# Changing the load order, the first norm's path and the last columns of a planned two-block kernel

## The chip, the cores and the metric

The kernel runs on one core of one Trainium2 chip. The metric is the device time of one execution in microseconds (us); 773.08 us is the median of the runs of the kernel before.

## The reference, cut to what matters

A sequence of 256 rows of width 1024 (x) goes through two transformer blocks in float32. The first block has two layers; each normalises x, projects it, runs several kinds of attention (global with rotary positions, windowed, neighbourhood, and attention to a memory of 256 rows), gates the result and adds an output projection. The second block has a mixer, a cross attention and a squared-ReLU MLP, and ends with a norm. Two places matter here. The first is the start of the first layer:

```
h = rmsnorm(x, norm_gain[0])                 # y = x * rsqrt(mean(x*x) + 1e-6) * g
qa, ka, va, qb, kb, vb, qm, gate = split_cols(h @ w_in_even, SPLIT_EVEN)
```

The second is the end of the MLP and the final norm:

```
x = x + squared_relu_mlp(rms_norm(x, g_mlp), w_up, w_down)
return rms_norm(x, g_final)
```

## The kernel before, in words

**Numbers.** Every float32 operand of a product is split in two: a high half, rounded to the fast float32 format (`t_wh` for weights, `t_gh`, `t_hT`, `t_mT`, `t_yh` for activations), written by ScalarE (ACT), and a low half, the remainder (`t_wl` and so on), written by VectorE (DVE). A product of two split operands is three matmuls, high by high, high by low and low by high (`mm3`), or two instructions where high and low activations stand side by side. So each load of weights (`t_raw`, three buffers of up to 1 MB, loaded over SP's queue) needs one instruction of ScalarE and one of VectorE before TensorE (PE; its weight loads are PEld) can finish with it, and a `raw` buffer comes free when VectorE has written the low half.

**Who sets the order.** The kernel's methods do not issue anything; `Plan.record` notes each instruction with what it depends on. `Plan.order` then plays the program through with a table of costs: at each step it takes the engine that can start earliest, and on it the ready instruction with the lowest priority number, which is the place in the program plus `bias`. A transfer is given 450 ns on its queue, and its bytes at 358 bytes per ns on one common bus. The engines and queues get their instructions in that fixed order, so a wrong guess of a time shows on the chip as an engine that waits although other work of its own is ready. `either` lets the plan choose between VectorE and ScalarE for one step. `nc.ahead` lets a load be issued ahead of its place.

**The start.** `consts` loads the gains and the first two 128-row blocks of x transposed (`xT`, host-made input `x_t`), one over SP's and one over ACT's queue, and gives PE 24 matmuls on zeros (`t_warm`). `layer_even` does not wait for the norm's factor r (one per row of x): it multiplies the columns of x.T by the gain alone (`gain_t`, whose `turn(k)` makes the two halves `t_gh` for one block of 128), and sums q, k, v and the second k's neighbours for k = 0 to 7, 896 columns in four PSUM banks (`sweep`; 12 matmuls for each k). The factor r is applied to these results afterwards. `columns` issues the loads of two k at a time in the pieces of its list: rows j0 to j1 and columns d0 to d1. Behind each pair of k stands a load of further blocks of x.T (`load_x`); with k = 6 come the rows of x themselves. `rope_tables` loads tables after k = 2 and 3.

From the rows of x, two sums of squares for each half (`square_sum`, either engine), the sum plus epsilon and a power of -1/2 on GpSimd (POOL) give r (`rstd`). All of this is recorded with `bias` -200, 200 places ahead. The products that follow (the second attention's k, called kb here, then the gate, then more) need the normed x transposed and split (`hT`). The kernel before gets it without a transpose of x: `spread` writes r on the diagonal of two 128x128 tiles (`t_p<-t_cst,t_rstd`), multiplies them by ones on PE (`t_at<-t_p,t_ones`) and copies the result, r along the free axis in every partition (`t_y`); VectorE then makes eight products x.T times gain times r (`t_xs`), and four pairs of instructions split them (`t_hT`).

`turns` is another way, used by later norms: the normed rows (`t_xn`, made by `scaled`, either engine) are transposed on PE in 128x128 pieces (`t_at<-t_cst,t_xn`), and ScalarE and VectorE evacuate each pair of pieces into the two halves with the gain (`t_mT`).

**The end.** `down_last` does the last product for each half of the rows (tt = 0, 1). For tt = 1 the second 512 columns are cut in two, and the last 256 go through a PSUM tile of their own (`own`). After each piece come the residual on VectorE (`t_x<-t_mm,t_rstd,t_x`), a sum of squares (`square_sum`) and the product with the final gain (`t_xg<-t_x,t_gb`). Then r from the sums (VectorE), the power (POOL), the scaling by r on VectorE and ScalarE, and the stores. The order of a piece's steps on VectorE there is again the plan's.

Of the kernel before, what the change touches and what calls it, by code (L numbers as in the profile page):

```python
# [10 lines left out]
F32 = mybir.dt.float32  # L11
# [5 lines left out]
P = 128  # L17
# [12 lines left out]
class Plan:  # L30
# [13 lines left out]
    def __init__(self, nc):  # L44
        import concourse.bacc as bacc
        self.nc = nc
        self.names = bacc.Bacc("TRN2", target_bir_lowering=False, num_devices=1)
        self.ops, self.tiles, self.last, self.bias, self.ahead, self.table = [], {}, None, 0, False, 0.0
        for e in self.ENGINES:
            setattr(self, e, Plan.Engine(self, e))  # L50

# [31 lines left out]
    def record(self, engine, method, args, kwargs):  # L83
        op = dict(i=len(self.ops), engine=engine, method=method, args=args, kwargs=kwargs, deps={}, uses=set(),
                  bias=self.bias)
        outs = [v for v in args[:1] if isinstance(v, bass.AP)] + [kwargs[k] for k in ("out", "accum_out") if k in kwargs]
        ins = [v for v in args[1:] if isinstance(v, bass.AP)]
        ins += [v for k, v in kwargs.items() if k not in ("out", "accum_out") and isinstance(v, bass.AP)]
        op["kind"] = self.tiles[outs[0].tensor.name]["kind"] if self.mine(outs[0]) else None
        for write, vs in ((False, ins), (True, outs)):  # L90
            for v in vs:
                if not self.mine(v):
                    continue
                t, b = self.box(v)
                op["uses"].add(t["name"])
                bank = t["pool"].space == bass.MemoryType.PSUM
                for j, w, c in t["log"]:
                    if j == op["i"] or not (w or write):
                        continue
                    o = self.ops[j]  # L100
                    if bank and engine == o["engine"] == "tensor":
                        op["deps"].setdefault(j, 0.0)
                    elif b[0] < c[1] and c[0] < b[1] and b[2] & c[2]:
                        lat = self.latency(o["engine"], engine) if engine != o["engine"] or w and not write else 0.0
                        op["deps"][j] = max(op["deps"].get(j, 0.0), lat)
                t["log"].append((op["i"], write, b))
        if engine == "tensor":
            self.last = op["i"]
        elif method == "dma_start" and op["kind"] != "raw" and self.last is not None and not self.ahead:
            op["deps"].setdefault(self.last, 0.0)  # L110
        op["cost"], op["after"], op["bytes"] = self.cost(engine, method, args, kwargs, outs, ins)
        op["forms"] = [(engine, method, args, kwargs, op["cost"])]
        self.ops.append(op)
# [48 lines left out]
    def order(self, prio):  # L162
# [37 lines left out]
        while len(seq) < n:  # L200
# [19 lines left out]
            if o["bytes"]:  # L220
                if e != "gpsimd":
                    ring[e] = max(ring[e], t) + 450.0
                    avail[e] = (ring[e], i)
                    bus = max(bus, ring[e] + 650.0)
                else:
                    bus = max(bus, end[i] + 650.0)
                bus += o["bytes"] / 358.0
                done = bus + o["after"]
            self.done[i] = done
            seq.append(i)  # L230
# [77 lines left out]
class Kernel:  # L308
# [59 lines left out]
    def consts(self):  # L368
# [9 lines left out]
        warm = self.base.tile([P, S], F32R, name="warm")  # L378
        nc.vector.memset(warm.bitcast(F32), 0.0)
        self.xT = [self.slot([P, 4, S], "xT", F32) for _ in range(2)]  # L380
        for k, queue in enumerate((nc.sync, nc.scalar)):
            self.load_x(k, 1, queue)
        busy = self.psum("at")
        for _ in range(WARM):
            nc.tensor.matmul(busy[:, 0, :], warm[:, :P], warm, start=True, stop=True)
# [133 lines left out]
    def gain_t(self, src, key, fast=False):  # L519

        nc = self.nc
        f = Halves(lambda: self.slot([P, 2, 2, S], "gh"))

        def turn(k):
            v, g, h, l = src[k // 4][:, k % 4, :], self.gcol(key, k), f(0, k), f(1, k)
            if k == 0 and fast:
                nc.vector.tensor_scalar(h, v, g, None, ALU.mult)
            else:
                nc.scalar.activation(h, v, AF.Copy, scale=g)
            nc.vector.scalar_tensor_tensor(l, v, g, h.bitcast(F32), ALU.mult, ALU.subtract)  # L530

        return f, turn
# [475 lines left out]
    def layer_even(self):  # L1008
# [5 lines left out]
        def columns(k0, parts, raw=None):  # L1014


            if raw is None:
                raw = self.wp.tile([P, 2, 896], F32, tag="raw", name=self.name("raw"), bufs=3)
            for j0, j1, d0, d1 in parts:
                c = d0 if d0 < 768 else d0 + 640  # L1020
                nc.sync.dma_start(raw[:, j0:j1, d0:d1], w_in[(k0 + j0) * P:(k0 + j1) * P, c:c + d1 - d0]
                                  .rearrange("(k p) c -> p k c", p=P))
# [12 lines left out]
                             k == 0, k == KT - 1)  # L1035

        for k0 in range(0, KT, 2):
            raw = columns(k0, ((0, 1, 0, 512), (0, 2, 512, 768), (0, 2, 768, 896), (1, 2, 0, 512)) if k0 == 0 else
                          ((0, 2, 0, 768), (0, 2, 768, 896)) if k0 < 6 else ((0, 1, 0, 768), (0, 1, 768, 896)))
            if k0 < 6:  # L1040
                self.load_x(k0 + 2, 2, nc.sync)
            else:
                for t in range(2):
                    nc.ahead = True
                    nc.sync.dma_start(self.x[:, t, :], a["x"][0, t * P:(t + 1) * P])
# [10 lines left out]
        for c in range(2):  # L1056
            squares(c)
        r = self.rstd(ms)
        rb = self.spread(r, self.work("y", [P, S], YB))
        hT = Halves(lambda: self.slot([P, 2, 2, S], "hT"))  # L1060
        for c in range(2):
            t = self.slot([P, 4, S], "xs", F32)
            for k in range(4):
                nc.vector.scalar_tensor_tensor(t[:, k, :], self.xT[c][:, k, :], self.gcol("norm0", 4 * c + k), rb,
                                               ALU.mult, ALU.mult)
            for k in (0, 2):
                self.hilo(*hT.pair(4 * c + k), t[:, k:k + 2])
        nc.bias = 0
        self.sink = self.base.tile([P, 8], F32, name="sink")
        nc.sync.dma_start(self.sink, a["sink_b"].to_broadcast([P, 8]))  # L1070
# [258 lines left out]
    def mlp(self, ms):  # L1329
# [47 lines left out]
        def down_last(s, t):  # L1377
            parts = [list(self.wide(a["w_down_2"], 512 * s, 4, 512 * c)) for c in range(2)]
            parts = [[(k0, *self.split(v)) for k0, v in half] for half in parts]
            for tt in range(2):  # L1380
# [4 lines left out]
                for i, (c, b0, b1) in enumerate(cuts):  # L1385
# [16 lines left out]
                    xv = self.x[:, tt, cs]  # L1402
                    if own:
                        nc.vector.scalar_tensor_tensor(xv, o, r2[:, tt:tt + 1], xv, ALU.mult, ALU.add)
                    self.square_sum(xv, ms[:, i:i + 1])
                    held.append((xg[c][:, tt, bs], xv, gb[:, cs]))
                    if b1 - b0 == 512:
                        nc.vector.tensor_tensor(*held.pop(), ALU.mult)
                r = self.work("rstd", [P, 2], 4)[:, :1]
                nc.vector.scalar_tensor_tensor(r, ms[:, 0:1], EPS, ms[:, 1:2], ALU.add, ALU.add)  # L1410
                if tt == 1:
                    nc.vector.tensor_tensor(r, r, ms[:, 2:3], ALU.add)
                nc.gpsimd.tensor_tensor(r, r, self.mhalf[:, :1], ALU.pow)
                for v in held:
                    nc.vector.tensor_tensor(*v, ALU.mult)
                rows = slice(tt * P, (tt + 1) * P)
                v = [xg[c][:, tt, :] for c in range(2)]
                nc.vector.tensor_scalar(v[0], v[0], r, None, ALU.mult)
# [140 lines left out]
```

## Time and profile before

| | |
|---|---|
| median of 3 runs | 773.08 us (772.73 to 773.56) |
| profiled execution | 773.77 us |
| its span in the profile | 771.9 us |
| mean granted TensorE clock | 0.997 |
| PE, DVE, ACT, POOL busy | 99%, 80%, 69%, 9% of the span |
| moved by the DMA queues | 140.39 MB, 182 GB/s in the mean |

A row of the timeline gives the start in us from the span's start, the duration (of several merged instructions: from the first start to the last end), the engine, the operation, what it writes and reads, shapes, the count, and in brackets the idle time before it and what ended that. All instructions have line 284, the line of `issue`, so the tile names tell the groups apart. Matmuls overlap, and their ends are modelled.

### The profile page before, as it was taken

Reading aid. Unit: us, or ns where it says so; the run is one execution under the profiler, and the core shown is the slowest. Engines: PE = TensorE matmul, PEld = TensorE weight load, DVE = VectorE, ACT = ScalarE, POOL = GpSimd, SP = SyncE. Lnnn points to the kernel's source line nnn. Section 1 sums busy time; section 2 is a strip of 40 time slices with the busy share of each in tenths; the row PEclk is TensorE's granted clock in tenths of the full one; section 3 lists DMA queues with packets and bytes.
Section 4 is the critical chain, followed back from the end, with each engine's and each line's share of the span. In section 5 each row is a group of like instructions: output and inputs, shape, how many; then the busy total and the mean of one; then the engine's idle time right before and its main releaser. Section 6 shows DMA issues by size and latency. Waiting matters only on the chain.

```text
span 771.9 us, 11841 instructions
## 1 busy us (share of the span) xinstructions
PE 760.7 (99%) x4370; PEld 662.6 (86%) x4370; DVE 614.3 (80%) x1136; ACT 529.0 (69%) x1034; POOL 66.6 (9%) x98
## 2 busy tenths in 40 slices
PE   9999999999999999999999999999999999999996
PEld 7898888888888888888888898899988888888885
DVE  5999998988779789979998899886677665555655
ACT  5687986976678678757796788466556765555562
POOL 2140010000001511132001000100000000000000
PEclk9999999999999999999999999999999999999998
DMA  8893555445568854765456644356535665656541
GB/s 315 284 268 111 165 183 177 159 165 164 164 211 250 218 188 144 199 197 193 134 191 194 191 163 156 117 165 219 191 110 164 195 188 167 204 177 209 170 163 55
DMA packets 109145, 140.39 MB, mean 182 GB/s; under 512 B 3744, under 2 KB 80736, under 8 KB 109088
## 3 DMA queue, kind: packets, MB, share of 16 engines
q1 hardware_dynamic: 103184, 131.12, 52.7%
q0 software_dynamic: 5472, 8.10, 4.8%
q8 instruction: 34, 0.56, 0.3%
q10 hardware_dynamic: 432, 0.43, 0.2%
q14 instruction: 23, 0.19, 0.1%
HBM read 134.92 MB, written 1.05 MB: 176 GB/s over the span
## 4 chain that ended last, share of the span: by engine, by line
PE 82%; ACT 6%; DVE 6%; DMA 3%; issue 2%; SPq 0%; POOLq 0%; POOL 0%; ACTq 0%; DVEq 0%
PE t_mm L284 61%; PE t_at L284 21%; DVE t_wl L284 2%; DMA t_raw<-in_w_in_even_dram 2%; ACT t_p L284 2%; ACT t_wh L284 2%; ACT t_y L284 1%; DVE t_y L284 1%; DVE t_p L284 1%; DMA t_xT<-in_x_t_dram 0%; ACT t_ph L284 0%; SPq L284 0%; ACT t_sum L284 0%; DVE t_pl L284 0%; DVE t_tanh L284 0%
## 5 line engine op out<-in xcount | busy, mean ns | idle before, releaser
L284 DVE TENSOR_TENSOR t_wl<-t_raw,t_wh 128x1024 fp32r<-128x1024 f32 (+2 forms) x238 | 288.7, 1217 | 69.9 <-ACT t_wh L284 67.2
L284 ACT ACTIVATE t_wh<-t_raw 128x1024 fp32r<-128x1024 f32 (+2 forms) x238 | 249.7, 1054 | 78.7 <-PE t_mm L284 57.4
L284 PE MATMUL t_mm<-t_mT,t_wh 128*128 128x512 f32 x496 | 179.6, 401 | 0.0
L284 PE MATMUL t_mm<-t_mT,t_wl 128*128 128x256 f32 x496 | 131.0, 283 | 0.0
L284 PE MATMUL t_mm<-t_wh,t_yh 128*128 128x512 f32 (+1 forms) x288 | 113.3, 393 | 0.0
L284 PE MATMUL t_mm<-t_wl,t_yh 128*128 128x512 f32 (+1 forms) x288 | 112.3, 390 | 0.0
L284 PE MATMUL t_mm<-t_wh,t_yl 128*128 128x512 f32 (+1 forms) x288 | 111.9, 391 | 0.0
L284 PEld LDWEIGHTS t_mm<-t_mT,t_wh 128*128 128x128 f32 x496 | 91.0, 188 | 13.4
L284 PEld LDWEIGHTS t_mm<-t_mT,t_wl 128*128 128x128 f32 x496 | 93.2, 189 | 6.6
L284 PE MATMUL t_at<-t_mT,t_wh 128*128 128x512 f32 x240 | 86.0, 395 | 0.0
L284 ACT COPY t_sum<-t_mm 128x256 f32<-128x256 f32 x90 | 33.2, 369 | 51.8 <-PE t_mm L284 51.3
L284 PE MATMUL t_mm<-t_wh,t_gh 128*128 128x256 f32 (+2 forms) x256 | 63.8, 333 | 0.0
L284 PEld LDWEIGHTS t_mm<-t_wl,t_yh 128*128 128x128 f32 x288 | 54.2, 188 | 10.7
L284 PEld LDWEIGHTS t_mm<-t_wh,t_yl 128*128 128x128 f32 x288 | 54.1, 188 | 10.6
L284 PEld LDWEIGHTS t_mm<-t_wh,t_yh 128*128 128x128 f32 x288 | 54.1, 188 | 10.3 <-ACT t_yh L284 0.3
L284 PE MATMUL t_at<-t_mT,t_wl 128*128 128x256 f32 x240 | 62.6, 280 | 0.0
L284 ACT ACTIVATE t_p<-t_p,t_st 128x256 f32<-128x256 f32 (+1 forms) x111 | 53.2, 494 | 10.6 <-DVE t_st L284 10.5
L284 PEld LDWEIGHTS t_at<-t_mT,t_wh 128*128 128x128 f32 x240 | 44.5, 188 | 8.3 <-issue 0.2
L284 DVE TENSOR_TENSOR t_sum<-t_mm,t_sum 128x256 f32<-128x256 f32 x90 | 37.9, 422 | 13.9 <-ACT t_sum L284 12.9
L284 PE MATMUL t_mm<-t_hT,t_wh 128*128 128x512 f32 (+1 forms) x160 | 48.3, 356 | 0.0
L284 PEld LDWEIGHTS t_at<-t_mT,t_wl 128*128 128x128 f32 x240 | 45.2, 188 | 3.5
L284 PE MATMUL t_mm<-t_gh,t_wh 128*128 128x512 f32 x128 | 47.3, 404 | 0.0
(189 smaller groups left out, 1371.7 us busy)
## 6 DMA issues: line engine op xcount, KB each, us to landing
t_raw<-in_w_in_odd_dram SPq DMA_DIRECT2D x20, 1024.0 KB, 5.2
t_raw<-in_w_up_dram SPq DMA_DIRECT2D x16, 1024.0 KB, 5.7
t_raw<-in_w_down_dram SPq DMA_DIRECT2D x16, 1024.0 KB, 5.0
t_raw<-in_w_in_dram SPq DMA_DIRECT2D x12, 1024.0 KB, 5.3
t_raw<-in_w_in_even_dram SPq DMA_DIRECT2D x10, 1024.0 KB, 5.1
t_raw<-in_w_mem_kv_dram SPq DMA_DIRECT2D x8, 1024.0 KB, 5.2
t_raw<-in_w_out_even_dram SPq DMA_DIRECT2D x6, 1024.0 KB, 5.2
t_raw<-in_w_out_odd_dram SPq DMA_DIRECT2D x6, 1024.0 KB, 5.9
```

Source lines behind the costliest of these rows:

```text
L284: f(*[self.real(v) for v in args], **{k: self.real(v) for k, v in kwargs.items()})
```

## The change

Five edits in one:

1. The second block of x.T is loaded over SP's queue, behind three pieces of the first weights, instead of over ACT's; `turn(1)`'s high half is made by VectorE.
2. The weights of k = 2 and 3 are loaded as k = 2's first 768 columns, the last 128 of both, then k = 3's, instead of both at once. The list of pieces now holds the loads of x.T as well (entries of two numbers).
3. `spread` and the products on x.T go. The rows of x are scaled by r and transposed as in `turns`.
4. In `down_last`, the sum of squares of the last 256 columns is fixed to VectorE; the first two sums are added at once; the product with the gain of those columns must come behind the sum that needs the square (`behind`, a dependence for the plan alone, on the last instruction recorded). The other 256 columns' product is recorded at once instead of behind the power.
5. The plan counts the transfers' bytes at 320 per ns instead of 358, for the whole program.

```diff
@@ Plan.record
+        if self.behind is not None:
+            op["deps"].setdefault(self.behind, 0.0)
@@ Plan.order
-                bus += o["bytes"] / 358.0
+                bus += o["bytes"] / 320.0
@@ consts
-        for k, queue in enumerate((nc.sync, nc.scalar)):
-            self.load_x(k, 1, queue)
+        self.load_x(0, 1, nc.sync)
@@ gain_t
-            if k == 0 and fast:
+            if k < 2 and fast:
                 nc.vector.tensor_scalar(h, v, g, None, ALU.mult)
             else:
                 nc.scalar.activation(h, v, AF.Copy, scale=g)
@@ layer_even, columns
-            for j0, j1, d0, d1 in parts:
+            for part in parts:
+                if len(part) == 2:
+                    self.load_x(*part, nc.sync)
+                    continue
+                j0, j1, d0, d1 = part
@@ layer_even
-            raw = columns(k0, ((0, 1, 0, 512), (0, 2, 512, 768), (0, 2, 768, 896), (1, 2, 0, 512)) if k0 == 0 else
-                          ((0, 2, 0, 768), (0, 2, 768, 896)) if k0 < 6 else ((0, 1, 0, 768), (0, 1, 768, 896)))
-            if k0 < 6:
-                self.load_x(k0 + 2, 2, nc.sync)
-            else:
+            raw = columns(k0, (((0, 1, 0, 512), (0, 2, 512, 768), (0, 2, 768, 896), (1, 1), (1, 2, 0, 512), (2, 2)),
+                               ((0, 1, 0, 768), (0, 2, 768, 896), (1, 2, 0, 768), (4, 2)),
+                               ((0, 2, 0, 768), (0, 2, 768, 896), (6, 2)),
+                               ((0, 1, 0, 768), (0, 1, 768, 896)))[k0 // 2])
+            if k0 == 6:
@@ layer_even
         r = self.rstd(ms)
-        rb = self.spread(r, self.work("y", [P, S], YB))
-        hT = Halves(lambda: self.slot([P, 2, 2, S], "hT"))
+        halves = [self.slot([P, 2, 512], "xn", F32) for _ in range(2)]
         for c in range(2):
-            t = self.slot([P, 4, S], "xs", F32)
-            for k in range(4):
-                nc.vector.scalar_tensor_tensor(t[:, k, :], self.xT[c][:, k, :], self.gcol("norm0", 4 * c + k), rb,
-                                               ALU.mult, ALU.mult)
-            for k in (0, 2):
-                self.hilo(*hT.pair(4 * c + k), t[:, k:k + 2])
+            for t in range(2):
+                self.scaled(halves[c][:, t, :], self.x[:, t, c * 512:(c + 1) * 512], r[:, t:t + 1])
+        hT = self.turns("n", halves, "norm0")
+        self.flush("n")
@@ down_last
-                    self.square_sum(xv, ms[:, i:i + 1])
+                    if own:
+                        junk = self.work("p", [P, 512], PB)[:, :b1 - b0]
+                        nc.vector.tensor_tensor_reduce(out=junk, in0=xv, in1=xv, scale=1.0 / D, scalar=0.0,
+                                                       op0=ALU.mult, op1=ALU.add, accum_out=ms[:, i:i + 1])
+                    else:
+                        self.square_sum(xv, ms[:, i:i + 1])
                     held.append((xg[c][:, tt, bs], xv, gb[:, cs]))
-                    if b1 - b0 == 512:
+                    if not own:
                         nc.vector.tensor_tensor(*held.pop(), ALU.mult)
-                r = self.work("rstd", [P, 2], 4)[:, :1]
-                nc.vector.scalar_tensor_tensor(r, ms[:, 0:1], EPS, ms[:, 1:2], ALU.add, ALU.add)
+                    if i == 1:
+                        r = self.work("rstd", [P, 2], 4)[:, :1]
+                        nc.vector.scalar_tensor_tensor(r, ms[:, 0:1], EPS, ms[:, 1:2], ALU.add, ALU.add)
                 if tt == 1:
                     nc.vector.tensor_tensor(r, r, ms[:, 2:3], ALU.add)
-                nc.gpsimd.tensor_tensor(r, r, self.mhalf[:, :1], ALU.pow)
+                nc.behind = len(nc.ops) - 1
                 for v in held:
                     nc.vector.tensor_tensor(*v, ALU.mult)
+                nc.behind = None
+                nc.gpsimd.tensor_tensor(r, r, self.mhalf[:, :1], ALU.pow)
```

More of the change, by code (lines that the diff above doesn't have):

```diff
@@ L47, in __init__ @@
         self.names = bacc.Bacc("TRN2", target_bir_lowering=False, num_devices=1)
-        self.ops, self.tiles, self.last, self.bias, self.ahead, self.table = [], {}, None, 0, False, 0.0
+        self.ops, self.tiles, self.last, self.bias, self.ahead, self.table, self.behind = [], {}, None, 0, False, 0.0, None
         for e in self.ENGINES:
```

## The prediction

> **What bounds the kernel now.** I read the page's first part first, the busy share of each engine.
>
> ```profile
> span 771.9 us, 11841 instructions
> PE 760.7 (99%) x4370; PEld 662.6 (86%) x4370; DVE 614.3 (80%) x1136; ACT 529.0 (69%) x1034; POOL 66.6 (9%) x98
> ```
>
> TensorE is the bound, and a busy share of 99% says that little idle time is to be had anywhere. So I asked the windows view where that little lies. Columns: the stretch, its length, then busy time (instructions) of PE, PEld, DVE, ACT and POOL, clock, DMA share, GB/s.
>
> ```profile
> 6.30:17.70 11.40, 10.77 (x51) 8.77 (x50) 6.74 (x11) 6.68 (x11) 4.08 (x12) 1.00 0.98 357
> 17.70:28.70 11.00, 9.56 (x47) 7.83 (x46) 10.40 (x23) 7.73 (x15) 0.82 (x1) 1.00 0.93 292
> 28.70:43.30 14.60, 14.56 (x117) 14.52 (x118) 13.55 (x33) 11.83 (x23) 3.69 (x6) 1.00 0.96 297
> 43.30:65.00 21.70, 20.84 (x158) 19.22 (x156) 21.01 (x44) 14.85 (x28) 7.16 (x7) 1.00 0.75 222
> 65.00:110.00 45.00, 44.78 (x270) 38.39 (x269) 44.04 (x83) 41.06 (x103) 0.00 (x0) 1.00 0.44 141
> ```
>
> One matmul of the kind that fills the third stretch, from the timeline (start, duration):
>
> ```profile
> 30.38 0.28 PE L284 MATMUL t_at<-t_hT,t_wl 128*128 128x256 f32 x1
> ```
>
> PE's idle time here is 0.63, 1.44, 0.04, 0.86 and 0.22 us, 3.2 us in all, nearly all of it before 65 us, and that is where the change works. The first stretch is bound by transfers (DMA share 0.98). From 17.7 us on VectorE is nearly full: 10.40 of 11.00, later 21.01 of 21.70. Idle time is counted from a matmul's modelled end. In the third stretch 117 matmuls, mostly of 256 columns, start every 0.125 us, while its row gives one 0.28 us. So a stall costs about 0.16 us more than its row says, and the true sum is nearer 5 us than 3.2.
>
> **Part 1: loads and first splits.** The timeline of PE, ACT and DVE names each stall and its releaser.
>
> ```profile
> 2.64 3.93 PE L284 MATMUL t_at<-t_warm 128*128 128x256 f32 x18
> 6.41 0.40 PE L284 MATMUL t_mm<-t_wh,t_gh 128*128 128x512 f32 x1
> 12.65 0.50 PE L284 MATMUL t_mm<-t_wl,t_gh 128*128 128x512 f32 x1 [0.63 <-DVE t_wl L284]
> 17.79 0.50 PE L284 MATMUL t_mm<-t_wl,t_gh 128*128 128x512 f32 x1
> 10.51 1.79 ACT L284 ACTIVATE t_wh<-t_raw 128x896 fp32r<-128x896 f32 x2 [2.04 <-DMA t_raw<-in_w_in_even_dram]
> 3.62 0.99 SPq L284 DMA_DIRECT2D t_raw<-in_w_in_even_dram  x2
> 15.65 1.80 ACT L284 ACTIVATE t_wh<-t_raw 128x896 fp32r<-128x896 f32 x2 [2.55 <-DMA t_raw<-in_w_in_even_dram]
> 16.64 2.09 DVE L284 TENSOR_TENSOR t_wl<-t_raw,t_wh 128x896 fp32r<-128x896 f32 x2 [2.11 <-ACT t_wh L284]
> ```
>
> Moving x.T's second block from ACT's queue to SP's, behind three weight pieces, lets the first weights land earlier, and the k = 1 product on VectorE frees ScalarE for their split. I cost this at nothing: the warm-up matmuls hold PE until 6.57 by the model, and the first real matmul starts at 6.41 whatever is ready sooner. That cover lasts as long as k = 0's two splits end before 6.4. SP gains two DMA issues (x.T's, and the third piece of k = 2 and 3). The queue of transfers is full behind them (0.98), so I take 0; the upper end is one issue time, 0.5 us (0.99 for two).
>
> Loading k = 2 alone first takes 128 x 768 x 4 B = 393 kB off its way, 1.1 us at 357 GB/s: its split could start at 9.4 instead of 10.51, and the 0.63 us at 12.65 goes. But what is late next is k = 4: its bytes, and all those ahead of it, are the same, so it lands at 15.6 and its low half is ready near 17.7, which is where PE resumes now (17.79). The stall moves from k = 2 to k = 4. I take 0. The bounds: -0.6 if a gap in the transfers closes (the 0.63 us kept), +0.5 if an extra issue delays k = 4.
>
> **Part 2: first normed x.** Removed are the two products that spread r over partitions, a copy, eight products on x.T and four pairs of split halves. Added are four row scalings, sixteen transposes and eight pairs of evacuations. The nearest rows for what is added are those of the second layer's norm, which does exactly this.
>
> ```profile
> 21.77 0.71 PE L284 MATMUL t_at<-t_p,t_ones 128*128 128x128 f32 x4 [0.56 <-DVE t_p L284]
> 22.23 0.47 PE L284 MATMUL t_mm<-t_wl,t_gh 128*128 128x512 f32 x1
> 27.63 2.01 ACT L284 ACTIVATE t_wh<-t_raw 128x1024 fp32r<-128x1024 f32 x2 [1.59 <-DMA t_raw<-in_w_in_even_dram]
> 28.74 0.51 PE L284 MATMUL t_at<-t_hT,t_wh 128*128 128x256 f32 x2 [0.92 <-ACT t_wh L284]
> 29.08 0.57 PE L284 MATMUL t_mm<-t_wh,t_gh 128*128 128x512 f32 x2
> 21.43 0.29 DVE L284 TENSOR_SCALAR t_p<-t_cst,t_rstd 128x128 f32<-128x128 f32 x1 [0.60 <-POOL t_rstd L284]
> 21.63 2.17 DVE L284 TENSOR_TENSOR t_wl<-t_raw,t_wh 128x896 fp32r<-128x896 f32 x2
> 23.71 2.06 DVE L284 SCALAR_TENSOR_TENSOR t_xs<-t_xT,t_gT,t_y 128x256 f32<-128x256 f32 x5
> 25.70 1.29 DVE L284 TENSOR_TENSOR t_hT<-t_xs,t_hT 128x512 fp32r<-128x512 f32 x2
> 26.90 1.27 DVE L284 SCALAR_TENSOR_TENSOR t_xs<-t_xT,t_gT,t_y 128x256 f32<-128x256 f32 x3
> 28.09 1.22 DVE L284 TENSOR_TENSOR t_wl<-t_raw,t_wh 128x1024 fp32r<-128x1024 f32 x1
> 194.64 1.28 DVE L284 TENSOR_SCALAR t_xn<-t_x,t_rstd 128x512 f32<-128x512 f32 x3 [0.84 <-POOL t_rstd L284]
> 195.70 1.69 PE L284 MATMUL t_at<-t_cst,t_xn 128*128 128x128 f32 x14
> 196.23 3.03 ACT L284 ACTIVATE t_mT<-t_at,t_gT 128x256 fp32r<-128x256 f32 x8 [0.65 <-PE t_at L284]
> 197.10 3.23 DVE L284 SCALAR_TENSOR_TENSOR t_mT<-t_at,t_gT,t_mT 128x256 fp32r<-128x256 f32 x8
> ```
>
> PE: the spread goes from 21.77 to 22.23, 0.46 us. Fourteen transposes in 1.69 us with 0.27 for the last are one every 0.11 us, so sixteen cost 1.75 us. PE's own work grows by 1.29 us, and nothing later hides it, since PE is full; it pays only in stalls. Two are at hand. At 21.77 PE waited 0.56 us for r, and r still comes from the same power on GpSimd; the transposes wait for the scaled rows instead. I keep half, 0.28. At 28.74 it waited 0.92 us for the gate's first weights, which landed about 27.6, and right behind it (29.08) came matmuls of the k sweep that had been free to run: the order had counted on earlier weights. The planner's transfer rate of 320 instead of 358 B/ns plans them later, so these matmuls come ahead and the wait goes. With 0.16 for each stall's hidden part, counted half for the first: +1.75 - 0.46 - 0.28 - 0.92 - 0.24 = -0.15 us. The transposed path's sixteen evacuations need the same PSUM buffers as the gate; both are four deep, and I cost that at nothing.
>
> VectorE: out go 0.29 + 2.06 + 1.27 + 2 x 1.29 = 6.2 us, in come 1.28 + 3.23 = 4.5 us (4.9 with the fourth scaling there too): 1.3 to 1.7 us less in a stretch where it is full. ScalarE's eight evacuations (3.03 us) take the place of its four halves of hT, and it has 3.3 us idle between 17.7 and 28.7. The k = 1 product is added before 6 us, where VectorE waits. What VectorE's relief is worth is bounded by PE's later stalls for it:
>
> ```profile
> 44.02 0.33 PE L284 MATMUL t_at<-t_cst,t_p 128*128 128x128 f32 x1 [0.42 <-DVE t_p L284]
> 51.78 0.39 PE L284 MATMUL t_mm<-t_hT,t_wl 128*128 128x256 f32 x1 [0.25 <-DVE t_wl L284]
> ```
>
> These two, with their hidden parts, are 1.0 us; the ends are 0 (the order made anew puts other waits there) and the relief of 1.5. I take 1.0, the two rows.
>
> The new rate reorders the rest of the program too. Behind 110 us no named stall is left that weights' arrival causes, so I take 0 and hold 0.5 us either way, the size of one such stall above.
>
> **Part 3: the last columns.** Rows of the tail, and two of the same GpSimd power elsewhere.
>
> ```profile
> 765.79 0.15 DVE L284 SCALAR_TENSOR_TENSOR t_rstd<-t_ms 128x1 f32<-128x1 f32 x1
> 765.91 0.42 DVE L284 TENSOR_TENSOR t_xg<-t_x,t_gb 128x256 f32<-128x256 f32 x1
> 766.51 0.16 DVE L284 TENSOR_TENSOR t_rstd<-t_rstd,t_ms 128x1 f32<-128x1 f32 x1 [0.18 <-ACT t_p L284]
> 766.75 0.56 POOL L284 TENSOR_TENSOR t_rstd<-t_rstd,t_mhalf 128x1 f32<-128x1 f32 x1 [4.55 <-DVE t_rstd L284]
> 393.42 0.69 DVE L284 CUSTOM_DVE_ANT_0 t_p<-t_xg 128x512 f32<-128x512 f32 x1
> 393.54 1.15 POOL L284 TENSOR_TENSOR t_rstd<-t_rstd,t_mhalf 128x2 f32<-128x2 f32 x1 [35.97 <-DVE t_rstd L284]
> 193.89 0.72 POOL L284 TENSOR_TENSOR t_rstd<-t_rstd,t_mhalf 128x2 f32<-128x2 f32 x1 [80.89 <-DVE t_rstd L284]
> ```
>
> The square of 512 columns takes VectorE 0.69 us, so of 256 about 0.42: 765.91 to 766.33, and the sum starts near 766.36 without the crossing from ScalarE, 0.15 us earlier. The product (0.42 us) now follows the sum at once, 0.12 behind its start as at 765.79 and 765.91, while the power starts 0.24 behind it (766.51 to 766.75). So the power runs beside a VectorE instruction with two tensors in SBUF. At 393.54 it did that, and took 1.15 us instead of 0.72: 0.43 more, with 0.57 us of the square left. Less 0.14, here with 0.30 left, that is 0.16 us. I take -0.15 + 0.16 = 0, between -0.15 (no contention) and +0.4 (the first sum is put ahead of the last residual and waits for ScalarE).
>
> The Trainium skill, "SBUF — State Buffer", section "Who interferes with whom", says that such a VectorE instruction and a GpSimd one that reads SBUF exclude each other for the whole instruction, whichever starts first. This speaks against the edit; the trace agrees in direction (0.43 of 0.57 us). By the rule the tail would be 0.15 us slower, by the rows even.
>
> **Sum.** 0 - 0.15 - 1.0 + 0 = -1.15 us. The profiled execution took 773.77 us, 1.87 beside its span of 771.9; the median of the runs is 773.08, 0.69 below, and the change is set against that: 772.0 us. 0.2% is 1.55 us, about what a measurement of this kernel can tell from no change, so this is within it.
>
> **Rivals.**
> (a) VectorE's relief carries on and the wait for the rows vanishes: 0.28 + 0.08 + 0.5 + 0.22 (the fifth stretch's idle) more, 1.1 us: 770.9. For it: kb's low half waited on VectorE until 28.09, and with it the release of a weight buffer. Against it: r is no earlier.
> (b) Slower. VectorE's eight evacuations are put ahead of k = 7's low half. From 21.43, scalings 1.28, k = 6's half 1.09, evacuations 3.23 and k = 7's half 1.09 end at 28.1. A step of k takes PE 2.4 us (two from 12.65 to 17.79, with the wait that ends there), so with the transposes until 24.1 it is done with k = 6 by 26.5 and then stands for 1.6 us. Against the forecast that is 1.6 + 0.92 + 0.16, and the full wait for r another 0.36: 775.0. It decides if those evacuations come first and no other matmul is ready. For it: norm instructions carry a priority 200 ahead. Against it: before, both halves (21.63) went ahead of the products all the same.
> (c) Nothing comes of the relief: PE's stalls only move, as at k = 4, 773.0.
>
> **How the numbers follow.** Forecast 0.48, with 771.3 to 773.0 its own range; (a) 0.32; (b) 0.13; (c) 0.07. Faster is (a) and 0.05 of the forecast, 0.37; slower is (b) less its mild end, 0.12; the rest 0.51. The range takes most of (a) and (b): 770.3 to 774.7.
>
> **What would show it.** Right: PE's stall at 12.65 gone and one of about 1 us at k = 4; sixteen transposes on PE between 22 and 26 us; no wait near 28.7; VectorE's stalls at 44 and 51 gone; the last power at about 0.7 us instead of 0.56. Wrong: k = 4's split starting well before 15.6, a stall ahead of k = 7, or new stalls behind 110 us.

## The result, and the profile after

The changed kernel takes 775.89 us (774.68 to 776.62), the kernel before on the same chip 773.45: a ratio of 1.0029, 95% interval 1.0018 to 1.0039. Measured again beside other kernels it took 775.11 against 773.59, 1.0024 (1.0014 to 1.0034). It is slower by 0.24 to 0.29%, where a gain of 1.15 us was forecast. Most runs of one kernel lie within 2 us of each other, and the profiled execution (774.68 us, span 772.9) is the fastest of its six: its trace shows about half of the loss.

The first part of the page after:

```profile
span 772.9 us, 11874 instructions
PE 762.0 (99%) x4382; PEld 664.7 (86%) x4382; DVE 615.0 (80%) x1142; ACT 528.8 (68%) x1029; POOL 65.2 (8%) x98
```

The windows view over the same five stretches as before:

```profile
6.30:17.70 11.40, 11.10 (x53) 9.43 (x53) 6.75 (x11) 6.15 (x10) 3.66 (x12) 1.00 1.04 361
17.70:28.70 11.00, 10.95 (x63) 9.64 (x62) 9.57 (x19) 9.44 (x21) 0.70 (x1) 1.00 0.87 279
28.70:43.30 14.60, 13.94 (x116) 13.74 (x114) 12.99 (x34) 11.51 (x21) 3.71 (x6) 1.00 1.00 308
43.30:65.00 21.70, 20.59 (x152) 18.83 (x152) 21.06 (x45) 14.87 (x27) 6.58 (x7) 1.00 0.73 227
65.00:110.00 45.00, 44.51 (x270) 38.42 (x270) 43.99 (x84) 40.38 (x100) 0.00 (x0) 1.00 0.43 141
```

PE's idle time went from 0.63, 1.44, 0.04, 0.86 and 0.22 us to 0.30, 0.05, 0.66, 1.11 and 0.49. So the first two stretches did gain 1.7 us, and the later three gave back 1.1. With the 1.3 us of work that the transposes add, these 104 us end 0.7 us later by this count, and the whole span is 1.0 us longer.

Where that begins is seen on the queues. First SP, POOL and DVE of the kernel before:

```profile
10.50 1.07 SPq L284 DMA_DIRECT2D t_x<-in_x_dram  x2
20.57 0.82 POOL L284 TENSOR_TENSOR t_rstd<-t_rstd,t_mhalf 128x2 f32<-128x2 f32 x1 [4.03 <-DVE t_rstd L284]
```

and of the changed one, with ACT's square of the late half of x:

```profile
10.88 0.34 SPq L286 DMA_DIRECT2D t_x<-in_x_dram  x1
11.62 0.95 SPq L286 DMA_DIRECT2D t_raw<-in_w_in_even_dram  x2
12.61 0.70 SPq L286 DMA_DIRECT2D t_x<-in_x_dram  x1
20.44 0.63 ACT L286 ACTIVATE t_p<-t_x 128x512 f32<-128x512 f32 x1 [0.26 <-DMA t_x<-in_x_dram]
22.55 0.70 POOL L286 TENSOR_TENSOR t_rstd<-t_rstd,t_mhalf 128x2 f32<-128x2 f32 x1 [6.42 <-DVE t_rstd L286]
23.29 0.88 DVE L286 TENSOR_SCALAR t_xn<-t_x,t_rstd 128x512 f32<-128x512 f32 x2 [0.88 <-POOL t_rstd L286]
```

The rows of x used to be issued together at 10.50. Now SP reaches them later, and k = 6's two pieces stand between the halves. The second half's square waits for its transfer, and the power that gives r starts 1.98 us later. TensorE and its feeders after:

```profile
7.75 0.95 ACT L286 ACTIVATE t_wh<-t_raw 128x896 fp32r<-128x896 f32 x1 [1.43 <-DMA t_raw<-in_w_in_even_dram]
9.88 0.50 PE L286 MATMUL t_mm<-t_wl,t_gh 128*128 128x512 f32 x1 [0.30 <-DVE t_wl L286]
12.42 0.40 PE L286 MATMUL t_mm<-t_wl,t_gh 128*128 128x512 f32 x1
16.04 1.79 ACT L286 ACTIVATE t_wh<-t_raw 128x896 fp32r<-128x896 f32 x2 [3.31 <-DMA t_raw<-in_w_in_even_dram]
18.16 0.50 PE L286 MATMUL t_mm<-t_wl,t_gh 128*128 128x512 f32 x1
24.09 1.08 DVE L286 TENSOR_TENSOR t_wl<-t_raw,t_wh 128x896 fp32r<-128x896 f32 x1
24.82 1.69 PE L286 MATMUL t_at<-t_cst,t_xn 128*128 128x128 f32 x14
28.41 0.41 PE L286 MATMUL t_at<-t_mT,t_wh 128*128 128x256 f32 x2
31.77 0.34 PE L286 MATMUL t_mm<-t_wh,t_gh 128*128 128x384 f32 x1
44.14 0.33 PE L286 MATMUL t_at<-t_cst,t_p 128*128 128x128 f32 x1 [1.49 <-DVE t_p L286]
43.80 0.28 DVE L286 TENSOR_TENSOR t_p<-t_p,t_tanh 128x128 f32<-128x128 f32 x1
```

TensorE does not stand at the transposes, since other products are put ahead of them. But k = 7's weights are split by 25.17 (24.09 + 1.08), and yet its last product, which the second row block's rope over k needs, starts at 31.77: 24 matmuls of the first projection (from 28.41) stand ahead of its last three. VectorE ends that rope at 44.08 (43.80 + 0.28), 0.11 us later than before. TensorE was 0.95 us ahead of the kernel before when it transposed the first block's rope (41.90 against 42.85), and it loses that lead here: it stands 1.49 us for the second. Before, the same wait was 0.42.

### The profile page after: what moved, and what is told of

The parts are those of the page before. It is cut to its first block, busy times and chain, and to the rows that moved or that the text cites. A ratio compares the mean times of both kernels' runs of the same rounds, so it can differ in the third digit from the quotient of the medians.

```text
span 772.9 us, 11874 instructions
## 1 busy us (share of the span) xinstructions
PE 762.0 (99%) x4382; PEld 664.7 (86%) x4382; DVE 615.0 (80%) x1142; ACT 528.8 (68%) x1029; POOL 65.2 (8%) x98
## 4 chain that ended last, share of the span: by engine, by line
PE 83%; DVE 7%; ACT 6%; DMA 2%; issue 1%; SPq 0%; POOLq 0%; POOL 0%; DVEq 0%; ACTq 0%
PE t_mm L286 62%; PE t_at L286 21%; ACT t_p L286 2%; DVE t_wl L286 2%; ACT t_wh L286 2%; DMA t_raw<-in_w_in_even_dram 2%; DVE t_p L286 1%; DVE t_y L286 1%; ACT t_y L286 1%; DVE t_x L286 0%; ACT t_ph L286 0%; SPq L286 0%; DVE t_pl L286 0%; DVE t_xg L286 0%; DVE t_tanh L286 0%
## 5 line engine op out<-in xcount | busy, mean ns | idle before, releaser
L286 PE MATMUL t_mm<-t_mT,t_wh 128*128 128x512 f32 (+1 forms) x656 | 227.9, 390 | 0.0
L286 PE MATMUL t_mm<-t_mT,t_wl 128*128 128x256 f32 x624 | 166.0, 284 | 0.0
L286 PEld LDWEIGHTS t_mm<-t_mT,t_wh 128*128 128x128 f32 x656 | 119.1, 189 | 15.6
L286 PEld LDWEIGHTS t_mm<-t_mT,t_wl 128*128 128x128 f32 x624 | 117.4, 189 | 8.0
L286 PE MATMUL t_at<-t_mT,t_wh 128*128 128x512 f32 (+1 forms) x320 | 101.0, 368 | 0.0
L286 PE MATMUL t_at<-t_mT,t_wl 128*128 128x256 f32 x280 | 74.0, 281 | 0.0
L286 PEld LDWEIGHTS t_at<-t_mT,t_wh 128*128 128x128 f32 x320 | 57.2, 189 | 8.3 <-issue 0.2
L286 PEld LDWEIGHTS t_at<-t_mT,t_wl 128*128 128x128 f32 x280 | 52.9, 189 | 3.4
L286 PEld LDWEIGHTS t_mm<-t_wh,t_gh 128*128 128x128 f32 x256 | 44.1, 190 | 3.7
```

The source lines that it names most:

```text
L286: f(*[self.real(v) for v in args], **{k: self.real(v) for k, v in kwargs.items()})
```

## Experiments

Times are medians; ratios are to the kernel before on the same chip. The diffs show only the lines that matter, some of them shortened.

**Each part alone, on the kernel before.** `a1` takes over only the loads with `turn(1)` on VectorE, `a2` only the rows and transposes, `a3` only the last columns, `a4` only the rate.

```diff
a1: load_x, columns, turn (k < 2)     a2: scaled, turns instead of spread
a3: down_last and behind              a4: - o["bytes"] / 358.0   + o["bytes"] / 320.0
```

> Before with the loads of part 1 alone (x.T's second block on SP, k = 2's weights ahead of k = 3's, k = 1's high half on VectorE). PE-work theory (sixteen transposes add 1.3 us of PE work, and the early stalls they were to fill come back as a wait for the rope of k): this part holds no transposes, so 0 to -0.5 us. Load-order theory (the second half of x's rows lands later and r with it): +0.5 to +1.5 us, with the power that makes r at 22.5 us instead of 20.6. Planner theory (the rate of 320 does it): 0.

> Before with the first norm by rows and transposes alone. PE-work theory: +1 to +2 us. Load-order and planner theories: 0 to -0.5 us, since VectorE has 1.5 us less to do.

> Before with the tail's edit alone. All theories: within 0.2 us of before; if GpSimd's power were not held up by the product beside it, -0.15 us.

> Before with the planner's rate of 320 alone. Planner theory: +1 to +2.5 us, with the stalls of the changed kernel behind 42 us. PE-work and load-order theories: 0 to -1 us, because the 0.92 us wait for the gate's first weights goes.

| | time, us | before | ratio (95%) |
|---|---|---|---|
| a1, loads | 775.38 | 773.63 | 1.0020 (1.0005 to 1.0034) |
| a2, transposes | 774.32 | 773.63 | 1.0010 (1.0001 to 1.0018) |
| a3, tail | 773.65 | 773.63 | 1.0000 (0.9989 to 1.0011) |
| a4, rate | 775.64 | 773.63 | 1.0023 (1.0013 to 1.0032) |

Three of the four cost by themselves, and together they would give +4.5 us, twice the change. In `a1` both halves of x go behind k = 6's pieces, and the power is as late as in the changed kernel:

```profile
13.27 0.92 SPq L284 DMA_DIRECT2D t_x<-in_x_dram  x2
22.34 0.70 POOL L284 TENSOR_TENSOR t_rstd<-t_rstd,t_mhalf 128x2 f32<-128x2 f32 x1 [5.11 <-DVE t_rstd L284]
```

In `a4` the power is on time (20.83), but the plan has all of k = 7's products ahead of the first projection, and TensorE then waits 2.30 us, until 29.95, for that projection's weights, split late. The wait is not the whole cost. The windows view of `a4` (columns as before; the clock is the third number from the end) shows a low granted clock behind it:

```profile
30.00:32.00 2.00, 2.00 (x11) 2.00 (x12) 1.59 (x3) 2.00 (x4) 0.00 (x0) 0.61 0.63 183
32.00:34.00 2.00, 2.00 (x12) 2.00 (x11) 2.00 (x6) 0.57 (x1) 0.00 (x0) 0.54 1.09 377
34.00:36.00 2.00, 2.00 (x19) 2.00 (x19) 0.65 (x2) 1.54 (x3) 0.00 (x0) 1.00 1.04 380
```

TensorE is busy in all three stretches, but does 11 and 12 matmuls in the first two and 19 in the third. The clock that is missing, 0.39 and 0.46 of 2 us each, is worth 1.7 us.

**One part undone, on the changed kernel.** `b1` is the changed kernel again, `b2` has the old rate, `b3` the old loads, `b4` the old spread.

```diff
b2: - o["bytes"] / 320.0   + o["bytes"] / 358.0
b3: as before: x.T's block on ACT's queue, old pieces, k == 0
b4: as before: spread, t_xs, hT
```

> The changed kernel once more, for its spread and a second profile. If its median lies 1 us or more above the first profiled execution because of a transfer that lands late in some executions, this profile (if it is a longer one) shows one PE stall more, of 1 us or more, behind a ScalarE split that waits for a transfer. If the first profile was typical, 774.7.

> The changed kernel with the planner's rate back at 358. If the single parts added up (loads +1.7, transposes +0.7, tail 0, rate +2.0, against +2.4 for all), taking the rate out would give +2.4 - 2.0 = +0.4. Planner theory: about that, +0.5. PE-work theory (what costs is the 1.3 us of transposes): still +1.5 or more.

> The changed kernel with the loads and first splits of before (part 1 undone). Load-order theory (the second half of x's rows comes behind k = 6's first weights, and r with it): r's power back near 20.6 us, the wait for the rope of k short, and +0.5 or less. PE-work theory: +1.5 or more.

> The changed kernel with the first norm by spread and products, as before (part 2 undone). PE-work theory: 1.3 us less than the changed kernel, +1 or less. Load-order and planner theories: as the changed kernel or more, +2.5 to +3.5, since VectorE has 1.5 us more to do.

| | time, us | ratio (95%) |
|---|---|---|
| b1, as changed | 775.11 | 1.0024 (1.0014 to 1.0034) |
| b2, old rate | 776.85 | 1.0045 (1.0032 to 1.0057) |
| b3, old loads | 773.15 | 0.9993 (0.9985 to 1.0002) |
| b4, old spread | 775.57 | 1.0023 (1.0013 to 1.0033) |

The old loads take the whole loss away, 2.0 us against `b1` and 2.7 against the first measurement. The rate, which costs 2.0 us alone, saves 1.0 to 1.7 with the new loads; the transposes cost nothing within the change (775.57 without them). In `b3` the power is back at 20.85. In `b2` it is at 21.43, 1.12 us sooner than in the changed kernel, and yet `b2` is the slowest of all: k = 7's last product starts at 32.54, TensorE waits 2.48 us for the rope of k, until 45.41, and the granted clock behind that is 0.76, 0.50 and 0.89 in the three stretches of 2 us from 44 on, again 1.7 us. So the time of r alone does not decide.

**Only the place of x's rows.** `c1` is the changed kernel with the loads of x's rows recorded ahead of k = 6's. `c4` is `b3`, with the plan told that the second half is not free to go before the first `raw` buffer is, which puts it behind k = 6's two pieces, as in the changed kernel.

```diff
c1 +            if k0 == 6:
   +                (the two loads of self.x, moved up)
                raw = columns(k0, ...)
c4 +                for o in nc.ops:
   +                    if first in o["uses"]:        # first: raw of k = 0, 1
   +                        nc.ops[-1]["deps"][o["i"]] = 260.0
```

> The changed kernel with one thing moved: both halves of x by rows are put on SyncE's queue ahead of the weights of k=6 and 7, where the changed kernel has the second half behind k=6's first two pieces. Theory A (the cost of the load order is that the row sums, and so r, come later): GpSimd's power on the row sums goes from 22.55 back to about 21.0, VectorE's first scaled rows from 23.29 to about 21.7, the 1.65 us wait of TensorE at 42.4 shrinks below 0.6, and the time falls from 775.1-775.9 to 773.0-774.0. Theory B (the new loads cost by themselves, through the weights of k=2 in two pieces and x.T's second block on the queue, whatever r does): it stays at 775.0-775.9. Theory C (each new plan of the order scatters by 1 to 2 us later on): r early, the wait near 42 gone, but the time not below 774.5, with the loss behind 60 us.

> The mirror image: the changed kernel with the old loads (773.15, power on the row sums at 20.85) with one thing moved, the second half of x by rows put behind k=6's first two pieces, as the changed kernel has it. Theory A: the power comes at 22.3-22.7, TensorE waits again for VectorE by over 1 us between 40 and 52, and the time rises to 774.5-775.5. Theory B: 773.0-773.5, since the weights' pieces and x.T's blocks are the old ones. Theory C: any time from 772.5 to 775.5, with the difference behind 60 us.

`c1`: 773.63 against 773.46, 0.9999 (0.999 to 1.0008). `c4`: 774.91, 1.0018 (1.0009 to 1.0027). So with all its new loads, rate and transposes the changed kernel is as fast as the one before once x's rows are issued first, and the place of half of x alone brings 1.8 us back onto `b3`. Rival B, that the new pieces cost by themselves, falls. But theory A's times for the power did not come, as SP, POOL and PE of `c1` and then of `c4` show:

```profile
11.11 1.05 SPq L286 DMA_DIRECT2D t_x<-in_x_dram  x2
21.71 0.71 POOL L286 TENSOR_TENSOR t_rstd<-t_rstd,t_mhalf 128x2 f32<-128x2 f32 x1 [5.34 <-DVE t_rstd L286]
29.32 0.34 PE L286 MATMUL t_mm<-t_wh,t_gh 128*128 128x384 f32 x1
43.61 0.33 PE L286 MATMUL t_at<-t_cst,t_p 128*128 128x128 f32 x1
```

```profile
12.35 0.33 SPq L286 DMA_DIRECT2D t_x<-in_x_dram  x1
21.71 0.71 POOL L286 TENSOR_TENSOR t_rstd<-t_rstd,t_mhalf 128x2 f32<-128x2 f32 x1 [5.46 <-DVE t_rstd L286]
31.12 0.34 PE L286 MATMUL t_mm<-t_wh,t_gh 128*128 128x384 f32 x1
44.25 0.33 PE L286 MATMUL t_at<-t_cst,t_p 128*128 128x128 f32 x1 [0.97 <-DVE t_p L286]
```

The power is at 21.71 in both, where 21.0 and 22.3 to 22.7 had been expected. What differs is the order on TensorE. In `c4`, as in the changed kernel, k = 7's last three products stand behind the first projection's 24 matmuls, and TensorE later waits for the rope; in `c1` they stand behind two. That the 1.3 us between the two medians are this order's is a guess: the two traces are of executions only 0.16 us apart (773.69, and 773.85, the fastest of `c4`), and `c4` has the old pieces of the weights as well. The next pair asks for the order alone.

**Only the place of those products.** `d1` is the changed kernel with one edge for the plan, `d2` is `c1` with the reverse edge.

```diff
d1 +        for o in nc.ops[at:]:                     # the first projection
   +            if o["engine"] == "tensor": o["deps"].setdefault(end, 0.0)   # end: k = 7's last product
d2 +        for i in range(end - 2, end + 1):
   +            nc.ops[i]["deps"][mm[23]] = 0.0       # behind that projection's 24th
```

> The changed kernel with one edge added to the planned order: the first projection out of the transposed x (24 matmuls of 128x256) may not start before the last product of k=7. In the changed kernel these 24 stand between k=7's products and its last three, which so start at 31.77 instead of about 28.9, though their weights were ready at 25.2. Loads, rate and the row sums' time (power at 22.55) stay. Theory D (that place of the three products is the cost: the second row block's rope over k, its transposes and what follows come late): the last product starts at 28.7-29.1, the 1.65 us wait of TensorE at 42.4 falls below 0.4, and the time falls from 775.1-775.9 to 773.2-774.4. Theory A (the late row sums themselves are the cost): the power stays at 22.5, so the time stays at 775 or above. Theory C (any new plan scatters): the wait goes but the time stays above 774.7, with the loss behind 60 us.

> The mirror image, on the kernel with x's rows loaded first (773.63, last product of k=7 at 29.32, power at 21.71): the last three products are put behind the 24 matmuls of the first projection, nothing else is asked for. Theory D: the last product starts at about 32, TensorE waits for VectorE over 1 us between 41 and 46, and the time rises to 774.7-775.9. Theory A: the row sums come as early as before, so 773.2-774.0. Theory C: any time from 773 to 776 with the difference behind 60 us.

`d1`: 774.57, 1.0012 (1.0003 to 1.0021), 0.5 to 1.3 us less than the changed kernel, with the power still at 22.59; its interval overlaps those of the changed kernel. `d2`: 774.46, 1.0014 (1.0005 to 1.0023), 0.8 above `c1`, with a wait of 0.47 us at 44.62 and not of over 1; its profiled execution has the power at 22.29, so a share of the 0.8 may be the row sums'. Both medians go the way of theory D, `d1` to just above its range and `d2` to just below it, so D is at most a part and not the whole. PE and POOL of `d1`:

```profile
43.22 0.33 PE L286 MATMUL t_at<-t_cst,t_p 128*128 128x128 f32 x1 [0.31 <-DVE t_p L286]
57.29 0.41 PE L286 MATMUL t_at<-t_cst,t_p 128*128 128x128 f32 x2 [1.55 <-DVE t_p L286]
46.33 2.07 POOL L286 DMA_DIRECT2D t_ks<-t_ks  x4 [8.14 <-ACT t_ks L286]
48.41 3.72 POOL L286 TENSOR_TENSOR t_rrs<-t_rrs,t_mhalf 128x8 f32<-128x8 f32 x2
```

The wait of 1.49 us fell to 0.31, and one of 1.55 came for q's rope: the power it needs stands on GpSimd behind four transfers, as it does in the changed kernel (47.56). In `c1` it goes ahead of them, at 43.71.

**The power ahead of the transfers.** `e1` is the changed kernel with that edge alone, `e3` has both edges.

```diff
+        for i in ks:                                  # the four transfers
+            self.ops[i]["deps"].setdefault(q, 0.0)    # q: q's first power
```

> The changed kernel with one edge added to the planned order on GpSimd's queue: the four transfers of k's stack that it issues at 45.18 to 47.56 go behind q's first power, which in the changed kernel waits behind them (its operand is ready at 45.37, it starts at 47.56). The place of k=7's last three products is left as it is. Theory E (besides the products, this place of the power is a second cost: q's rope comes about 4 us late, 55.75 instead of 51.3-52.4): the power starts at about 45.4, q's first rope ends near 53, the wait at 42.4 stays at 1.5-1.7, and the time falls by 0.4 to 1.2, to 774.2-775.1. Rival (nothing waits for q's rope that early, the three products are the whole cost): 775.1-775.9 as before.

> The changed kernel with both edges: k=7's last three products ahead of the first projection (774.57 by itself) and q's first power ahead of the four transfers of k's stack. The loads stay the changed kernel's, the row sums' power stays at 22.5. Theory D with E: the wait at 42.4 stays below 0.5, the wait of 1.71 at 55.46 goes, and the time falls to 773.0-774.1, that of the kernel with x's rows first (773.63). Rival 1 (the late row sums keep a share of the cost): 774.3-775. Rival 2 (a new plan scatters by itself): any time up to 776 with new waits behind 60 us.

`e1`: 774.42, 1.0012 (1.0003 to 1.0020), inside theory E's range, with the wait at 44 still there. `e3`: 774.45, 1.0011 (1.0002 to 1.0020). Both intervals overlap those of the changed kernel, and the two edges do not add up. A wait for q's rope is left even with both, here at 54.25, and 0.8 us remain to `c1`. PE of `e1`, then of `e3`:

```profile
44.35 0.33 PE L290 MATMUL t_at<-t_cst,t_p 128*128 128x128 f32 x1 [1.50 <-DVE t_p L290]
```

```profile
54.25 0.41 PE L290 MATMUL t_at<-t_cst,t_p 128*128 128x128 f32 x2 [1.32 <-DVE t_rstd L290]
```

**Only the row sums later.** In `f1` and `f2` one or two powers with exponent 1 follow r's power on GpSimd in `c1`, costed at nothing in the plan: the order of every engine is that of `c1` but for them.

```diff
 r = self.rstd(ms)
+nc.gpsimd.tensor_tensor(r, r, ones[:, :2], ALU.pow)   # f2: twice
+nc.ops[-1]["cost"] = 0.0
```

> The kernel with x's rows first (773.63, row sums' power at 21.71) with one more power, to the exponent 1, behind the power on the row sums on GpSimd, costed at nothing in the plan: the order on every engine is the same but for this instruction, and everything that needs the row sums comes about 0.7 us later, as late as in the changed kernel (22.55). Theory A (late row sums cost by themselves, in any order): VectorE's first scaled rows at 23.1-23.3 instead of 22.45, waits of TensorE between 24 and 60 us grow by 0.5-0.8, and the time rises to 774.1-774.5. Rival (only the order that the plan makes of the loads costs): TensorE waits at most 0.2 more, 773.5-773.9.

> The same with two such powers, so the row sums come about 1.4 us later than in the kernel with x's rows first, in the same order of every engine. Theory A: 774.7-775.3, twice the rise of the single power. Rival: 773.5-774.1, since what TensorE does until 28.7 needs no row sums.

`f1`: 774.63, 1.0016 (1.0008 to 1.0025). `f2`: 775.62, 1.0027 (1.0016 to 1.0037). That is 1.0 and 2.0 us above `c1` for 0.7 and 1.5 us of GpSimd, a bit more than theory A's 0.5 to 0.9 and 1.1 to 1.7. Against the kernel before on each chip, `c1`, `f1` and `f2` are at +0.17, +1.35 and +2.34 us. POOL and PE of `f1`, then of `f2`:

```profile
22.09 0.70 POOL L286 TENSOR_TENSOR t_rstd<-t_rstd,t_ones 128x2 f32<-128x2 f32 x1
23.37 1.87 PE L286 MATMUL t_at<-t_cst,t_xn 128*128 128x128 f32 x15 [0.65 <-DVE t_xn L286]
```

```profile
22.86 1.48 POOL L286 TENSOR_TENSOR t_rstd<-t_rstd,t_ones 128x2 f32<-128x2 f32 x2
24.91 1.98 PE L286 MATMUL t_at<-t_cst,t_xn 128*128 128x128 f32 x16 [1.15 <-DVE t_xn L286]
```

In this order TensorE waits for the rows at once, where `c1` starts the same transposes at 22.99 without a wait. The waits of 0.65 and 1.15 us are less than what the medians rose by. In these two executions TensorE also stood 1.21 and 1.62 us between 6.3 and 17.7 instead of `c1`'s 0.63, which a power behind 21 us cannot cause, so their traces do not give the whole of the 1.0 and 2.0. In the changed kernel the plan, which knows of the late rows, puts k = 6's and 7's products there; TensorE does not wait at 24, but its elementwise engines start as late, and the wait comes at 44.

**Where the loss is complete.** The power of the second layer's norm, at 193.89 before, is a mark in every trace. It is at 194.54 and 194.65 in the two traces of the changed kernel, at 193.25 in `c1` and 192.49 in `b3`. So the whole distance from these two is there by then, and theory C, which puts it behind 60 us without the early waits, is not needed for them. With the edges it is at 194.50 (`d1`), 194.39 (`e1`) and 194.16 (`e3`), a gain of 0.0 to 0.5 us. The mark is only as good as one execution: it comes at 192.75 in `a3`, whose order is that of the kernel before up to there.

## Why the prediction was wrong, step by step

**The step that failed is Part 1**, "I take 0; the upper end is one issue time". It followed the weights and TensorE's first stalls and stopped there. Of the queue it counted two more issues, but not who stands behind them: x's rows. The loads alone cost 1.75 us (`a1`), and inside the change 2.0 to 2.7 (775.11 and 775.89 against `b3`'s 773.15). "r still comes from the same power" and "r is no earlier" took r's time as given; it came 1.98 us later. The row that says so is the power's on GpSimd. With x's rows issued first, the other edits kept and the order planned anew, the loss is gone (`c1`). How r's lateness becomes the loss is shown in part. In `c1`'s order, later row sums by themselves cost 1.0 us for 0.7 and 2.0 for 1.5 (`f1`, `f2`). In the changed kernel's own order the path through VectorE, which is nearly full behind r (21.06 of 21.70 us) and so hands a late start on, is argued from the wait at 44. The order that the plan makes of the new loads puts k = 7's last products and q's power late; without the one, the other or both (`d1`, `e1`, `e3`) the medians are 0.5 to 0.7 us below `b1` and 1.3 to 1.5 below the first measurement, which is not clear of the noise.

**Part 1, the stalls.** In part as told. The stall for k = 2's low half is gone, as forecast: it starts at 12.42 without a wait. A new one of 0.30 us stands at 9.88, for k = 1's low half. The last piece of its weights now goes behind x.T's block, ScalarE splits it only at 7.75, and the cover by the warm-up matmuls was worked out for k = 0 alone. k = 4's split starts at 16.04, as said near 15.6, and its stall is 0.21 us at 18.16 by the starts of the matmuls, not 1 us.

**Part 2, TensorE's own time**: right in the work. Sixteen transposes between 24.4 and 26.5, the fourteen in 1.69 us; the wait near 28.7 gone; no wait for r at all where half had been kept. TensorE's idle time in the second stretch fell from 1.44 to 0.05 us, which with the spread's 0.46 about pays for the transposes' 1.75. But the 0.92 us for the gate's first weights, with 0.16 hidden, was one execution's. In `a3`, whose order on every engine is the same there, ScalarE and TensorE make the same split and the same products sooner and without a wait:

```profile
25.82 1.99 ACT L286 ACTIVATE t_wh<-t_raw 128x1024 fp32r<-128x1024 f32 x2
27.56 0.39 PE L286 MATMUL t_at<-t_hT,t_wh 128*128 128x256 f32 x2
```

So as far as two traces tell, this term was not there to be won in every execution. Without it TensorE's sum in Part 2 is +0.93 instead of -0.15.

**Part 2, VectorE's relief, -1.0**: wrong in the changed kernel. The waits at 44 and 51 were to go; the first is 1.49 us, since the relief of 1.3 to 1.7 us came behind a start 1.9 us later (scaled rows at 23.29 instead of `t_p` at 21.43). Where r is less late (20.85 in `b3`, 21.71 in `c1`) the wait at 44 does go, but one of 0.89 and 0.78 us stands at 50.56 and 51.32 for a weight split of the memory. These kernels come to -0.4 and +0.2 us, within what the measurement resolves, so a gain of 1.0 is not shown even there.

**The rate, 0 +- 0.5**: wrong in size, both ways: +2.0 alone (`a4`), -1.0 to -1.7 with the new loads (`b2`). No stall of its own was named for it because none stood in the trace before; the orders made anew had waits of 2.30 (`a4`) and 2.48 us (`b2`), each with 1.7 us of clock lost behind it.

**Part 3**: right in its total, 773.65 against 773.63 alone, which resolves no tenths of a us, and lucky in its terms. DVE and POOL of the tail after:

```profile
766.87 0.42 DVE L286 CUSTOM_DVE_ANT_0 t_p<-t_x 128x256 f32<-128x256 f32 x1
767.34 0.16 DVE L286 TENSOR_TENSOR t_rstd<-t_rstd,t_ms 128x1 f32<-128x1 f32 x1
767.42 0.42 DVE L286 TENSOR_TENSOR t_xg<-t_x,t_gb 128x256 f32<-128x256 f32 x1
767.64 0.60 POOL L286 TENSOR_TENSOR t_rstd<-t_rstd,t_mhalf 128x1 f32<-128x1 f32 x1 [4.48 <-DVE t_rstd L286]
768.28 0.68 DVE L286 TENSOR_SCALAR t_xg<-t_xg,t_rstd 128x512 f32<-128x512 f32 x2 [0.45 <-POOL t_rstd L286]
```

The square takes the 0.42 us that was worked out. From the last matmul's start (766.03, before 765.07) the sum comes 0.13 us sooner. The power starts 0.30 behind it instead of 0.24 and takes 0.60 instead of 0.56, so 0.10 us of the gain goes where 0.16 was said, and the scaling starts 2.25 us behind that matmul instead of 2.27. The power was to take about 0.7 us and did not; a later start, which the forecast did not have, took the most. The Trainium skill ("SBUF — State Buffer", "Who interferes with whom") would have the power wait while VectorE's product runs, until 767.84, 0.20 us. This trace does not agree: the power takes 0.04 us more than before, and with its later start 0.10 us are lost.

**The rivals.** The slower one, at 775.0, was near in time and wrong in kind: no eight evacuations stood ahead of k = 7's low half, which was ready at 25.17. What was missed lay beside it, k = 7's products themselves put late on TensorE.

**The sums.** Three slips change little. 773.08 - 1.15 is 771.9 and not 772.0. The five stalls that the rows name add 0.8 us of hidden part to the 3.2, which makes 4.0 and not nearly 5. Two steps of k from 12.65 to 17.79 are 2.57 us each and not 2.4, which puts rival (b) 0.2 us lower.

**What stays open.** Late row sums cost 1.0 and 2.0 us in `c1`'s order; in the changed kernel's own order their share was not measured apart from the order, which the plan makes from them. Why the plan puts the first projection ahead of the three products was not followed; it also does so with the old rate (`b2`, last product at 32.54) and in `a2` (32.62).

## What to carry to other kernels

Of a load that is moved, follow everything behind it on its queue to the first engine that needs it, and ask above all for the load that starts the longest chain (here x's rows), not only for the one that the bound engine waits for next. Where the engines behind such a chain are nearly full, do not price a late start at nothing because the bound engine has other work at that moment: here 0.7 and 1.5 us cost 1.0 and 2.0 (`f1`, `f2`), and in the changed kernel the wait came 20 us later under another name. Before a stall is booked as a gain, look whether a second trace of the same order has it. Where a planner makes the order, a change of its costs or loads is a new order, its parts do not add up (here +4.5 us alone, +1.5 to 2.4 together), and a range of half a microsecond for it was four times too narrow.

## What the runs showed of the hardware that was not expected

A power on GpSimd (128x1) beside a VectorE product of 256 columns takes 0.60 us in every kernel with the new last columns and 0.55 to 0.56 in every one with the old; a power (128x2) beside a square of 512 columns had taken 1.15 instead of 0.72.

A wait of TensorE of about 2 us can cost twice. Behind the waits of 2.30 us (`a4`) and 2.48 us (`b2`) the granted clock was low for some 4 us, worth 1.7 us each time. It happened a third time, in the profiled execution of `a3`. There a load ended ScalarE's wait only at 508.21, 5.03 us behind the split ahead of it, where the kernel before has 2.88 us. The scaled rows queued behind it, and TensorE stood 1.92 us:

```profile
508.21 1.06 ACT L286 ACTIVATE t_wh<-t_raw 128x1024 fp32r<-128x1024 f32 x1 [3.36 <-DMA t_raw<-in_w_q_mem_dram]
509.94 1.47 PE L286 MATMUL t_at<-t_cst,t_xn 128*128 128x128 f32 x6 [1.92 <-ACT t_xn L286]
```

The granted clock is 0.51 from 510 to 512 and 0.63 from 512 to 514, again 1.7 us. In the other traces no clock below 1.00 is seen ahead of the last 6 us, and their longest wait behind the first matmul is 1.55 us (`d1`). `a3`'s median is that of the kernel before, so one profile's total is no measure of such a kernel, and a single wait in it can be that execution's alone. The order of the instructions is the kernel's.
